# A two-layer hybrid decoder on one core: constants behind the first weights, later transposes at the seam, early products four pairs at a time

## Chip, core and metric

The kernel runs on one core of a Trainium2 chip. The metric is the time on the device of one launch, in microseconds (us). Five engines each work through an instruction list of their own, in order: PE (TensorE, matmuls and transposes), DVE (VectorE), ACT (ScalarE), POOL (GpSimd) and SP (SyncE, which here issues every DMA). A wait of an instruction holds up everything behind it in its engine's list.

## What is computed

Two layers over 1024 tokens of width 1024, in float32. Cut to what matters here:

```
h = RMSNorm_pre(x);  z = h @ W_in                  # conv group and attention group share one projection
m = concat(conv_out, attn_out) @ W_out
x = x + RMSNorm_post(m)                            # the mixer ends here
f = gated MLP(RMSNorm_pre(x)): up 1024 -> 2*2816, causal depthwise conv (3 taps), gate, down 2816 -> 1024
x = x + RMSNorm_post(f)
```

## The kernel before

**Arithmetic.** Every matmul operand is split in two parts, a rounded one and the rest, and every product is three matmuls (`prod`: high by high, low by high, high by low). Weights are loaded by SP into `raw` tiles and split by ACT (the high part) and POOL or DVE (the low part): in the mixer at L459 (load), L463 (ACT) and L469 (POOL), in the up stage at L1409 (load) and in `parts` (L1304, L1305).

**Mixer.** A planner (`Flow`, `fl`) runs Python generators on its own clock and writes the instructions of PE, DVE, ACT and POOL in the order in which it lets them go on; `yield 7.0` means that a generator goes on at about 7 us of that clock. At the start of layer 0 the eight row tiles of x (128 tokens each) are loaded (`first_x`, L242), normalised (`prenorm`: square on ACT L357, a power on POOL L349, scaling on DVE L359) and transposed by PE (L364); ACT copies the high part out of PSUM (L366) and DVE subtracts the low one (L367). A tile k takes two PSUM buffers, and there are two, so that tile k+1 is transposed when DVE has done with tile k. The tiles of x sit in buffers with the tags "y" and "xr", two of each.

**SP's order** is not written by hand. A scheduler places the DMAs by priority, and SP takes them one by one.

**The seam.** The up stage multiplies the normalised rows by 22 pairs of weight tiles in a scheme of seven products for four blocks. One product is a slot: four groups of three matmuls of 128x512, twelve in all. The list `seq` gives the order of slots as pairs (j, n), with j the product and n the weight pair. The right-hand sides are b11 and b21 (tokens of the first half, ready early), b22 (second half), and t1 to t4 (sums of blocks). Eight of the 22 pairs (`EARLY`) have their two products by b11 and b21, "e1" and "e2", put first of all, since those need no token of the second half. e2 adds to the PSUM bank that e1 has left: `e_copy` copies the bank to SBUF (tile `ea`, tag "acc", three buffers) after each of the two, and the copies are stored to DRAM (L1465), to be fetched when their pair's turn comes. Meanwhile the mixer's last four row tiles are finished: on DVE the residual sum (L1172, L1173), on ACT the square (L1178), on POOL the power, on DVE the scaling (L1185, tile `xn`). At the slots `NORM_T` `norm_t` transposes one of these four tiles each on PE (L1357), and in that slot and the three after it `norm_c` makes b22 and t1 to t4 of it: copies out of PSUM by ACT (L1374, L1375), subtractions by DVE (L1372, L1386), high parts by ACT (L1385, L1391). The first slots after the sixteen early ones are (1, 0), which takes the PSUM bank `pO`, and (6, 0), which reads t2.

```
L54    NORM_T = (2, 5, 8, 11)
L55    ACC_BUFS = 3
L1339  seq = [(j, n) for q in range(0, len(early), 2) for j in ("e1", "e2") for n in early[q:q + 2]]
L1459  def e_copy(n, j):
L1461      eh[n] = up.tile([P, T], F32, tag="acc", name="ea", bufs=ACC_BUFS)
L1462      se.activation(eh[n][:, 0:HB], px[n], AF.Copy)
L1465      sy.dma_start(esp[l][n], eh.pop(n))
L1619  px[n] = (pmm.tile([P, HB], F32, tag="mm", name="px") if j == "e1" else
```

PSUM pools: `pmm` has two banks, `pS` three, `ptr` two, `pO` one.

Of the kernel before, what the change touches and what calls it, by code (L numbers as in the profile page):

```python
# [17 lines left out]
P = 128  # L18
D = 1024
T = 1024  # L20
# [30 lines left out]
B_AHEAD = 8  # L51
F_AHEAD = 5
P_AHEAD = 3
NORM_T = (2, 5, 8, 11)  # L54
ACC_BUFS = 3  # L55
E_BUFS = 5
LATE = 12
# [156 lines left out]
def build(tc, ap, out):  # L214
# [7 lines left out]
    with ExitStack() as top:  # L222
# [14 lines left out]
        def const(name, shape, dt=F32):  # L237
            return cst.tile(shape, dt, tag=name, name=name)
# [9 lines left out]
            return t  # L248

        xin = [ap["x"][t * P:(t + 1) * P, :] for t in range(8)]  # L250
        first_x = lambda t: load_x(xin[t], ("y", "y", "xr")[t % 3])
        x0 = [first_x(0)]
        ident = const("ident", [P, P])
        sy.dma_start(ident, ap["ident"])
        identr = const("identr", [P, P], mybir.dt.bfloat16)
        ve.tensor_copy(identr, ident)
        g_pre = gvec(0, 0)
        x0 += [first_x(1), first_x(2)]
        nmask = xs.tile([P, P], F32, tag="m0", name="nmask", bufs=4)
        sy.dma_start(nmask, ap["nmask"])  # L260
        nmaskr = const("nmaskr", [P, P], mybir.dt.bfloat16)
        ve.tensor_copy(nmaskr, nmask)
        cos = const("cosT", [P, 8, 8])
        sy.dma_start(cos, ap["cos"])
        sin = const("sinT", [P, 8, 8])
        sy.dma_start(sin, ap["sin"])
        negh = const("negh", [P, 8])
        ve.memset(negh, -0.5)

        def params(l):  # L270

            li = 0.8 - 0.6 * math.exp(-0.3 * l)

            def ptile(key, shape):
                return par.tile(shape, F32, tag=key, name=f"{key}{l}", bufs=2)

            cw, cv, sg = ptile("cw", [P, 4, CK]), ptile("cv", [P, 3, 4]), ptile("sg", [P, 1])
            sy.dma_start(cw, ap["cw"][l])
            sy.dma_start(cv, ap["cvec"][l])
            sy.dma_start(sg, ap["subg"][l])  # L280
            lv = par.tile([P, 4, HD], F32, tag="lv", name="lv", bufs=1)
            sy.dma_start(lv, ap["lamv"][l:l + 1].broadcast_to([P, 4, HD]))
            cws, hv, ls, nl = ptile("cws", [P, 4, (CK + 1) // 2]), ptile("hv", [P, 2, 4]), ptile("ls", [P, 2]), ptile("nl", [P, 1])
            pars[l] = dict(cw=cw, cws=cws, cv=cv, hv=hv, sg=sg, nl=nl)
            yield
            ve.tensor_scalar(cw, cw, 0.5, None, op0=ALU.mult)
            ve.tensor_copy(cws[:, :, 0], cw[:, :, 0])
            cw2 = cw[:, :, 1:CK].rearrange("p c (m two) -> p c two m", two=2)
            ve.tensor_tensor(cws[:, :, 1:], cw2[:, :, 0], cw2[:, :, 1], op=ALU.add)
            ve.tensor_scalar(hv, cv[:, 1:3, :], 0.5, None, op0=ALU.mult)  # L290
            ve.tensor_scalar(sg, sg, (1.0 - li) * math.sqrt(P), None, op0=ALU.mult)
            ve.tensor_tensor(lv[:, 0:2, :], lv[:, 0:2, :], lv[:, 2:4, :], op=ALU.mult)
            ve.tensor_reduce(ls, lv[:, 0:2, :], axis=AX.X, op=ALU.add)
            se.activation(ls, ls, AF.Exp)
            ve.tensor_tensor(nl, ls[:, 1:2], ls[:, 0:1], op=ALU.subtract)
            ve.tensor_scalar(nl, nl, -li, None, op0=ALU.add)
# [117 lines left out]
        for l in range(DEPTH):  # L414
            xres = xin if l == 0 else x2[l - 1]
            with ExitStack() as st:
# [3 lines left out]
                hh = (hA, hB)  # L420
                if l == 0:
                    for t in range(8):
                        late[t] = prenorm(ptr, x0[t] if t < 3 else first_x(t), g_pre, hh[t // 4], t % 4)
                if l == 0:
                    for _ in params(0):
                        pass
                p = pars[l]
                wm = ap["wmix"][l]

# [840 lines left out]
                def next_params():  # L1270
                    g = params(l + 1)
                    yield 200.0
                    next(g)
                    yield 220.0
                    next(g, None)
                    fl.op("dve", 1.6)

                if l + 1 < DEPTH:
                    fl.spawn(next_params())
                with tc.manual_schedule(engines={mybir.EngineType.PE, mybir.EngineType.DVE,  # L1280
# [4 lines left out]
            with ExitStack() as st:  # L1285
# [44 lines left out]
                with ExitStack() as su:  # L1330
# [5 lines left out]

                    order = [i for k in range(K2) for i in (k, k + K2)]
                    early = EARLY
                    seq = [(j, n) for q in range(0, len(early), 2) for j in ("e1", "e2") for n in early[q:q + 2]]  # L1339
                    for n in range(NFT):  # L1340
                        if n in early:
                            seq += [(4, n - 1)] + [(j, n) for j in (6, 5, 7, 3)]
# [114 lines left out]
                            sy.dma_start(C[n][0][:, h0], esp[l][n][:, HB:T])  # L1457

                    def e_copy(n, j):  # L1459
                        if j == "e1":  # L1460
                            eh[n] = up.tile([P, T], F32, tag="acc", name="ea", bufs=ACC_BUFS)  # L1461
                            se.activation(eh[n][:, 0:HB], px[n], AF.Copy)  # L1462
                        else:
                            se.activation(eh[n][:, HB:T], px[n], AF.Copy)  # L1464
                            sy.dma_start(esp[l][n], eh.pop(n))  # L1465

                    def sums_of(n, j):
                        cg, cv = C[n]
# [144 lines left out]
                    for s, (j, n) in enumerate(seq):  # L1613
# [2 lines left out]
                        if s in before:  # L1616
                            norm_t(before[s])
                        if j in (1, "e1"):
                            px[n] = (pmm.tile([P, HB], F32, tag="mm", name="px") if j == "e1" else  # L1619
                                     pO.tile([P, HB], F32, tag="o", name="px"))  # L1620
                        elif j == 6:
                            py[n] = pS.tile([P, HB], F32, tag="S", name="py")
                        elif j == 5:
                            pz[n] = pS.tile([P, HB], F32, tag="S", name="pz")
# [237 lines left out]
```

## Time and profile before

| | us |
|---|---|
| median of 3 runs | 2316.41 (2315.09 to 2317.93) |
| the profiled execution | 2314.21 |
| its span in the trace | 2312.4 |
| PE busy | 2202.4 (95% of the span) |
| DVE busy | 1879.3 (81%) |
| ACT busy | 1126.7 (49%) |
| POOL busy | 832.6 (36%) |

The mean granted TensorE clock was 0.979 of full speed. The seam of layer 0 runs from about 497 to 554 us, that of layer 1 from 1644 to 1701 us. Of the waits of PE, the one that the words of this case speak of at the seam is that for the transposes (line L1357), and at the start that for the first transposes (line L364).

### The profile page before, as it was taken

To read this page: it belongs to the slowest core of one execution; us is meant where nothing else is said; L and a number is where in the kernel's file an instruction comes from. 1 tells how busy PE (TensorE), PEld (TensorE's weight loads), DVE (VectorE), ACT (ScalarE), POOL (GpSimd) and SP (SyncE) were. 2 spreads that over 40 slices of the span, in tenths; PEclk is the share of its full clock that TensorE was granted. 3 is DMA by queue.
4 is the path that set the end of the run, shared out by engine and by line. 5 is a ranking of instruction groups with operands and counts; after the bars stand their busy time and mean duration, and the time that the engine had idled before them with its cause. 6 is when DMAs were issued, how large, how long until landed. Compare 5 with 4: busy or idle time off the path is not lost. (4 is left out here: it accounts for less than half of the span.)

```text
span 2312.4 us, 31516 instructions
## 1 busy us (share of the span) xinstructions
PE 2202.4 (95%) x10568; PEld 1838.5 (80%) x10568; DVE 1879.3 (81%) x3287; ACT 1126.7 (49%) x2458; POOL 832.6 (36%) x894
## 2 busy tenths in 40 slices
PE   6999997999999999999889999979999999999998
PEld 5898895878877878788778988868788778787886
DVE  6988988667888888777889889896678888887777
ACT  4445456655444444444534545465554444445443
POOL 3324312245444545201533333122454554442024
PEclk9999997999999999999999999979999999999999
DMA  4313323454333343933433123235533343348353
GB/s 156 86 48 92 79 72 123 164 206 138 119 120 130 111 137 130 316 96 111 135 100 103 41 82 97 73 114 191 194 118 124 119 136 123 104 168 274 96 164 118
DMA packets 140129, 295.39 MB, mean 128 GB/s; under 512 B 16832, under 2 KB 33984, under 8 KB 139456
## 3 DMA queue, kind: packets, MB, share of 16 engines
q1 hardware_dynamic: 139968, 293.39, 39.7%
q8 instruction: 83, 1.36, 0.3%
q14 instruction: 78, 0.64, 0.1%
HBM read 198.44 MB, written 78.12 MB: 120 GB/s over the span
## 5 line engine op out<-in xcount | busy, mean ns | idle before, releaser
L1660 PE MATMUL pd<-wp,wo 128*128 128x512 f32 x1776 | 414.2, 395 | 4.8 <-DVE wp L1305 2.8
L1660 PEld LDWEIGHTS pd<-wp,wo 128*128 128x128 f32 x1776 | 333.9, 188 | 81.7 <-DVE wp L1305 3.6
L1609 PE MATMUL py<-t,wo 128*128 128x512 f32 x1584 | 381.8, 394 | 5.8 <-DVE cg L1477 5.8
L1609 PEld LDWEIGHTS py<-t,wo 128*128 128x128 f32 x1584 | 296.8, 188 | 77.4 <-ACT wo L1304 9.0
L1305 POOL TENSOR_TENSOR wo<-ws,wo 128x512 fp32r<-128x512 f32 x176 | 249.9, 1432 | 279.5 <-ACT wo L1304 274.1
L1609 PE MATMUL px<-hA,wo 128*128 128x512 f32 x1056 | 255.3, 394 | 0.0
L1305 POOL TENSOR_TENSOR wo<-raw,wo 128x512 fp32r<-128x512 f32 x132 | 181.4, 1378 | 166.1 <-ACT wo L1304 157.3
L1609 PEld LDWEIGHTS px<-hA,wo 128*128 128x128 f32 x1056 | 198.6, 189 | 44.5 <-ACT ea L1464 0.5
L1305 POOL TENSOR_TENSOR wo<-fa,wo 128x512 fp32r<-128x512 f32 x66 | 103.1, 1577 | 323.0 <-ACT wo L1304 293.9
L1304 ACT ACTIVATE wo<-ws 128x512 fp32r<-128x512 f32 x176 | 108.8, 627 | 136.7 <-PE py L1609 47.4
L1495 DVE SCALAR_TENSOR_TENSOR acc<-cg,fw,acc 128x512 f32<-128x512 f32 x176 | 132.6, 754 | 41.7 <-ACT acc L1483 38.1
L597 DVE SCALAR_TENSOR_TENSOR scr<-u,cw,scr 128x256 f32<-128x256 f32 (+2 forms) x288 | 158.0, 565 | 3.7 <-ACT scr L591 3.6
L852 ACT ACTIVATE e<-S,mxv 128x512 f32<-128x512 f32 (+2 forms) x192 | 110.1, 581 | 64.6 <-DVE mxv L847 41.2
L1483 ACT ACTIVATE acc<-cg,fb,fw 128x512 f32<-128x512 f32 x88 | 68.2, 774 | 148.8 <-DVE cg L1477 148.8
L857 POOL TENSOR_TENSOR sm<-sm 128x1 f32<-128x1 f32 x64 | 25.5, 398 | 316.9 <-ACT e L852 301.6
L499 PE MATMUL pq<-whq,hA 128*128 128x384 f32 x512 | 135.5, 346 | 3.9 <-ACT whq L463 3.9
L499 PE MATMUL pq<-whq,hB 128*128 128x384 f32 x512 | 133.9, 342 | 0.0
L1609 PE MATMUL pz<-b,wo 128*128 128x512 f32 x528 | 129.8, 394 | 1.9 <-DVE cv L1477 1.9
L1609 PE MATMUL pz<-t,wo 128*128 128x512 f32 x528 | 128.7, 392 | 0.0
L1609 PEld LDWEIGHTS pz<-b,wo 128*128 128x128 f32 x528 | 98.4, 188 | 27.4 <-issue 5.1
L843 DVE TENSOR_REDUCE mxv<-S 128x1 f32<-128x512 f32 (+2 forms) x192 | 100.5, 549 | 24.1 <-PE S L827 18.2
L1609 PEld LDWEIGHTS pz<-t,wo 128*128 128x128 f32 x528 | 99.1, 188 | 22.7
(279 smaller groups left out, 5027.2 us busy)
## 6 DMA issues: line engine op xcount, KB each, us to landing
raw<-in_wupd SPq DMA_DIRECT2D x104, 512.0 KB, 3.6
fa<-f SPq DMA_DIRECT2D x154, 256.0 KB, 2.7
f<-fs SPq DMA_DIRECT2D x88, 256.0 KB, 3.3
raw<-in_wmix SPq DMA_DIRECT2D x80, 256.0 KB, 3.0
f<-gg SPq DMA_DIRECT2D x66, 256.0 KB, 2.0
raw<-in_wmix SPq DMA_DIRECT2D x64, 192.0 KB, 2.4
qs<-sth SPq DMA_DIRECT2D x64, 128.0 KB, 2.4
os<-onT SPq DMA_DIRECT2D x16, 512.0 KB, 3.2
```

The lines of the kernel that those rows point to most:

```text
L499: mm = pe.matmul(dst, a, b, start=first and k + j == 0, stop=final and k == n - 1 and j == 2)
L597: ve.scalar_tensor_tensor(dst, src, wk, dst, op0=ALU.mult, op1=ALU.add)
L843: ve.tensor_reduce(mv_[:, j:j + 1], S, axis=AX.X, op=ALU.max, negate=True)
L852: se.activation(e[:, c0:c0 + w], S, AF.Exp, bias=mv_[:, 0:1], accum_out=sm[:, j:j + 1])
L857: po.tensor_tensor(sm[:, 0:1], sm[:, 0:1], sm[:, 1:2], op=ALU.add)
L1304: se.activation(w[:, 0], raw, AF.Copy)
L1305: eng.tensor_tensor(w[:, 1], raw, f32(w[:, 0]), op=ALU.subtract)
L1483: se.activation(acc[n, v, hf], C[n][v][:, 2 + hf * HB:2 + hf * HB + HB], AF.Identity, bias=fb[:, mt:mt + 1], scale=fw[:, mt, 2:3])
L1495: ve.scalar_tensor_tensor(dst, c[:, j + hf * HB:j + hf * HB + HB], fw[:, mt, j:j + 1], a, op0=ALU.mult, op1=ALU.add)
L1609: pe.matmul(ps, x, y, start=first and k + j == 0, stop=k == 3 and j == 2, skip_group_check=not first)
L1660: pe.matmul(ps[tt], x, y, start=first and k + n == 0, stop=k == K2 - 1 and n == 2, skip_group_check=not first)
```

## The change

Three things. **At the start**, the loads of `nmask`, `cos`, `sin` and of the layer's parameters are taken out of the row of first loads and put into a generator `constants` of the mixer's planner; the tiles of x go round "y", "y", "xr", "xr", so that four are loaded at once. **At the seam**, `NORM_T` moves to slots 4, 6, 9 and 12. **The early products** come in groups of four pairs in place of two, in four PSUM banks (two of `pmm`, one of `pO`, one of `pS`), and each `e_copy` takes an "acc" buffer of its own for half a tile and stores 256 KB itself: 16 stores of 256 KB in each layer in place of 8 of 512 KB.

```diff
-NORM_T = (2, 5, 8, 11)
+NORM_T = (4, 6, 9, 12)
...
-        first_x = lambda t: load_x(xin[t], ("y", "y", "xr")[t % 3])
+        first_x = lambda t: load_x(xin[t], ("y", "y", "xr", "xr")[t % 4])
...
-        x0 += [first_x(1), first_x(2)]
-        nmask = xs.tile([P, P], F32, tag="m0", name="nmask", bufs=4)
-        sy.dma_start(nmask, ap["nmask"])
+        x0 += [first_x(1), first_x(2), first_x(3)]
+        nmask = const("nmask", [P, P])
         nmaskr = const("nmaskr", [P, P], mybir.dt.bfloat16)
-        ve.tensor_copy(nmaskr, nmask)
         cos = const("cosT", [P, 8, 8])
-        sy.dma_start(cos, ap["cos"])
         sin = const("sinT", [P, 8, 8])
-        sy.dma_start(sin, ap["sin"])
...
                 if l == 0:
-                    for _ in params(0):
-                        pass
+                    par0 = params(0)
+                    next(par0)
...
+                def constants():
+                    yield 1.0
+                    next(par0)
+                    sy.dma_start(cos, ap["cos"])
+                    sy.dma_start(sin, ap["sin"])
+                    sy.dma_start(nmask, ap["nmask"])
+                    yield 7.0
+                    next(par0, None)
+                    ve.tensor_copy(nmaskr, nmask)
+                    fl.op("dve", 1.8)
+
+                if l == 0:
+                    fl.spawn(constants())
...
-                    seq = [(j, n) for q in range(0, len(early), 2) for j in ("e1", "e2") for n in early[q:q + 2]]
+                    seq = [(j, n) for q in range(0, len(early), 4) for j in ("e1", "e2") for n in early[q:q + 4]]
...
                     def e_copy(n, j):
-                        if j == "e1":
-                            eh[n] = up.tile([P, T], F32, tag="acc", name="ea", bufs=ACC_BUFS)
-                            se.activation(eh[n][:, 0:HB], px[n], AF.Copy)
-                        else:
-                            se.activation(eh[n][:, HB:T], px[n], AF.Copy)
-                            sy.dma_start(esp[l][n], eh.pop(n))
+                        e = up.tile([P, T], F32, tag="acc", name="ea", bufs=ACC_BUFS)[:, 0:HB]
+                        se.activation(e, px[n], AF.Copy)
+                        sy.dma_start(esp[l][n][:, 0:HB] if j == "e1" else esp[l][n][:, HB:T], e)
...
                         if j in (1, "e1"):
-                            px[n] = (pmm.tile([P, HB], F32, tag="mm", name="px") if j == "e1" else
-                                     pO.tile([P, HB], F32, tag="o", name="px"))
+                            q = early.index(n) % 4 if j == "e1" else 2
+                            px[n] = ((pmm if q < 2 else pO if q == 2 else pS)
+                                     .tile([P, HB], F32, tag=("mm", "mm", "o", "S")[q], name="px"))
```

The generator `params` is cut in three by one more `yield`: its tiles, its four loads, its arithmetic. The lines of the kernel move by a few numbers (L1609 becomes L1617, L1357 becomes L1368, L1462 and L1464 become L1472, L1465 becomes L1473).

PE at the seam of layer 0, before (px are the early products, hA_5273 is b11 and hA_5274 is b21, pt the transposes):

```order
1760 L1609 MATMUL px<-hA_5273,wo 128x512 x24
1761 L1357 MATMUL pt<-ident,xn 128x128 x8
1762 L1609 MATMUL px<-hA_5274,wo 128x512 x24
1763 L1609 MATMUL px<-hA_5273,wo 128x512 x12
1764 L1357 MATMUL pt<-ident,xn 128x128 x8
```

and now:

```order
1760 L1617 MATMUL px<-hA_5273,wo 128x512 x48
1761 L1368 MATMUL pt<-ident,xn 128x128 x8
1762 L1617 MATMUL px<-hA_5274,wo 128x512 x24
1763 L1368 MATMUL pt<-ident,xn 128x128 x8
1764 L1617 MATMUL px<-hA_5274,wo 128x512 x24
1765 L1617 MATMUL px<-hA_5273,wo 128x512 x12
1766 L1368 MATMUL pt<-ident,xn 128x128 x8
```

The first transposes stood behind two early products and stand behind four.

ACT at the same place, before (xn<-xe are the squares, ea<-px the copies of early products, ts and b_5734 the first copies of the transposed tile 0):

```order
430 L1178 ACTIVATE xn,ss<-xe 128x1024 x4
431 L1462 ACTIVATE ea<-px 128x512
432 L1304 ACTIVATE wo<-raw 128x512
433 L1462 ACTIVATE ea<-px 128x512
434 L1374 ACTIVATE ts<-pt 128x512
435 L1375 ACTIVATE b_5734<-pt 128x4x128
```

and now:

```order
433 L1175 ACTIVATE xn,ss<-xe 128x1024 x4
434 L1472 ACTIVATE ea<-px 128x512
435 L1315 ACTIVATE wo<-raw 128x512
436 L1472 ACTIVATE ea<-px 128x512
437 L1315 ACTIVATE wo<-raw 128x512
438 L1472 ACTIVATE ea<-px 128x512
439 L1315 ACTIVATE wo<-raw 128x512
440 L1472 ACTIVATE ea<-px 128x512
441 L1385 ACTIVATE ts<-pt 128x512
442 L1386 ACTIVATE b_5734<-pt 128x4x128
```

Four copies of early products, not two, stand ahead of the copies of tile 0.

SP at the same place, before (gb_0_10737 is the gain vector of the next layer, x_0_7 the last row tile's store):

```order
150 L1175 DMA x_0_7_113<-xe 128x1024
151 L247 DMA gb_0_10737<-in_norms 128x1024
152 L1409 DMA raw<-in_wupd 128x1024
153 L1465 DMA e_1_329<-ea 128x1024
154 L1465 DMA e_4_332<-ea 128x1024
```

and now:

```order
147 L1172 DMA x_0_7_111<-xe 128x1024
148 L247 DMA gb_0_10753<-in_norms 128x1024
149 L1473 DMA e_1_327<-ea 128x512
150 L1420 DMA raw<-in_wupd 128x1024
151 L1473 DMA e_4_330<-ea 128x512
152 L1473 DMA e_7_333<-ea 128x512
```

The first early store moves up past one load of weights, and still stands behind the load of the gain vector.

## Rows read from the trace of the kernel before

**Rows 1.** PE's waits: line waited for, us in total, times, longest.
```profile
PE pt L364 <- DVE ss L347: 13.7, 1, 13.7
PE pt L1357 <- DVE ss L347: 7.8, 2, 3.9
PE pq L499 <- POOL wlq L469: 3.8, 9, 0.6
```

**Rows 2.** Timeline, PE, layer 0's seam: start, us, engine, line, operation, count, idle before.
```profile
507.19 1.94 PE L1357 MATMUL pt<-ident,xn 128*128 128x128 f32 x8 [3.88 <-DVE ss L347]
508.79 9.31 PE L1609 MATMUL px<-hA,wo 128*128 128x512 f32 x36
...
527.12 1.03 PE L1357 MATMUL pt<-ident,xn 128*128 128x128 f32 x8
527.91 8.42 PE L1609 MATMUL px<-hA,wo 128*128 128x512 f32 x36
...
553.71 2.96 PE L1609 MATMUL py<-t,wo 128*128 128x512 f32 x12
```

**Rows 3.** Windows: stretch, us, busy by engine (count), granted clock, DMA share, GB/s.
```profile
505.00:510.00 5.00, 2.81 (x11) 2.64 (x12) 4.63 (x8) 4.60 (x10) 3.50 (x4) 0.71 0.73 297
```

**Rows 4.** Timeline, PE, layer 1's seam.
```profile
1644.81 5.60 PE L1609 MATMUL px<-hA,wo 128*128 128x512 f32 x24
...
1700.66 2.96 PE L1609 MATMUL py<-t,wo 128*128 128x512 f32 x12
```

**Rows 5.** Timeline, DVE: last scaling and first subtractions of the seams.
```profile
510.46 2.30 DVE L1185 SCALAR_TENSOR_TENSOR xn<-xe,rs,gb 128x1024 f32<-128x1024 f32 x1 [0.43 <-POOL rs L349]
512.69 0.68 DVE L1372 TENSOR_TENSOR ts<-pt,hA 128x512 f32<-128x512 f32 x1
...
1659.79 0.68 DVE L1372 TENSOR_TENSOR ts<-pt,hA 128x512 f32<-128x512 f32 x1
```

**Rows 6.** Timeline, ACT, layer 0's seam.
```profile
506.94 0.58 ACT L1462 ACTIVATE ea<-px 128x512 f32<-128x512 f32 x1
...
543.49 1.67 ACT L1385 ACTIVATE t<-ts 128x512 fp32r<-128x512 f32 x3
...
546.92 0.62 ACT L1304 ACTIVATE wo<-ws 128x512 fp32r<-128x512 f32 x1
```

**Rows 7.** DMA, 505 to 525 us (median us to landing), then all early stores.
```profile
e<-ea SPq DMA_DIRECT2D x2, 512.0 KB, 6.1
...
gb<-in_norms SPq DMA_DIRECT2D x1, 512.0 KB, 4.7
...
DMA to landing us min/median/max: 2.6/3.1/7.3
```

**Rows 8.** Timeline, SP's DMA issues, layer 0's seam.
```profile
512.79 0.33 SPq L247 DMA_DIRECT2D gb<-in_norms  x1
...
513.69 2.59 SPq L1465 DMA_DIRECT2D e<-ea  x2
```

**Rows 9.** Timeline, DVE, then PE, the start of the kernel.
```profile
11.37 0.23 DVE L262 CAST nmaskr<-nmask 128x128 bf16<-128x128 f32 x1 [6.62 <-DMA nmask<-in_nmask]
...
12.39 1.28 DVE L359 SCALAR_TENSOR_TENSOR xr<-xr,rs,gb 128x1024 f32<-128x1024 f32 x1 [0.73 <-POOL rs L349]
...
17.60 1.28 DVE L367 TENSOR_TENSOR hA<-pt,hA 128x512 fp32r<-128x512 f32 x2
...
13.73 1.97 PE L364 MATMUL pt<-ident,xr 128*128 128x128 f32 x8 [13.73 <-DVE ss L347]
...
25.13 1.67 PE L364 MATMUL pt<-ident,xr 128*128 128x128 f32 x8 [2.44 <-DVE hA L367]
...
28.40 1.12 PE L364 MATMUL pt<-ident,xr 128*128 128x128 f32 x4 [0.38 <-DVE hA L367]
```

**Rows 10.** DMA, issues from 0 to 4 us (median us to landing).
```profile
xr<-in_x SPq DMA_DIRECT2D x3, 512.0 KB, 7.8
gb<-in_norms SPq DMA_DIRECT2D x1, 512.0 KB, 6.9
```

## What I expect, and why

> **What bounds the kernel.** I first read the waits of PE, which is busy for 95% of the span, so that only what PE waits for can be won. The reader is to see three lines that the change touches [rows 1]: 13.7 us before the first transposes of the kernel, 7.8 us in two waits of 3.9 before the first transposes of each seam, and 3.8 us for split weights in the first projections. Then I read PE's timeline through the seam of layer 0 [rows 2]. After two early slots PE stands still for 3.88 us until the first of the four late row tiles is scaled, transposes it, and works on until (6, 0), the first product with t2, starts at 553.71. I use the start of (6, 0) as the mark of each seam. The wait has an after-effect: in the window from 505 to 510 us the mean granted clock is 0.71 of full speed [rows 3], so that after the idle time the lower of the two levels (1.2 and 2.4 GHz) was granted for a part; the eight transposes take 1.94 us there and 1.03 later, and 36 matmuls 9.31 us and later 8.42 [rows 2]. That is 0.9 + 0.9 = 1.8 us beside the 3.88. Layer 1's seam, from its first early product at 1644.81 to (6, 0) at 1700.66 [rows 4], has the other wait of 3.9.
>
> Behind PE runs a second chain. The sums b22 and t1 to t4 are made on DVE, tile after tile. DVE's subtractions of tile 0 start when the last row tile has been scaled, at 510.46 + 2.30 = 512.76 [rows 5], and from there DVE goes on with little idle time to t2 of tile 3. In layer 1 the same subtraction starts at 1659.79 [rows 5], 1147.10 later; both seams are copies of each other up to here.
>
> **Part 1, the transposes later, the four banks, in layer 1.** PE needs nothing of the second half for four slots. A slot is 12 matmuls, 8.42 / 36 x 12 = 2.81 us; four transposes take 527.91 - 527.12 = 0.79 each [rows 2]. Sixteen early slots, (1, 0) and four transposes without a wait are 17 x 2.81 + 4 x 0.79 = 51.0 us, against 1700.66 - 1644.81 = 55.85 [rows 4]: at most 4.8 us are won, the wait and the slower clock together. The number of matmuls, transposes and copies stays. But now DVE's chain is next. (1, 0) takes the bank that e2 of pair 17 had, and the copy of that stands on ACT behind the high parts of t1 to t3 of tile 3 and one more weight split. In layer 0 these high parts run from 543.49 for 1.67 us, and the split of a weight sum ends at 546.92 + 0.62 = 547.54 [rows 6]; the weight sums stand further ahead on DVE now, so I let the split end 1.5 us earlier, at 546.0, and the copy (0.58, as the one at 506.94) at 546.6. (1, 0) then runs from 546.6 and (6, 0) starts at 546.6 + 2.8 = 549.4. In layer 1 that is 549.4 + 1147.1 = 1696.5, a gain of 4.2. I take **-4.2** for layer 1. This holds if DVE's chain starts as before, at 1659.79; ACT's four copies must be through by then. The fourth copy needs the buffer of the first, so it waits until the first half tile is stored. The first copy ends at about 1654.6 (506.94 + 0.58 + 1147.1), and a store takes 3.1 us as the median of all early stores [rows 7]: 1657.8, one copy and the copies of tile 0 behind it, 1659.4. It just fits. With the longest landing, 7.3 [rows 7], it would be 4.2 us later, DVE's chain 3.6 behind what it was, and the gain 0.6; without any wait it is 4.8.
>
> **Part 2, the same seam in layer 0, with a new wait.** Here SP's list differs: ahead of the first early store stands the load of the next layer's gain vector, which overwrites one that the last scaling reads. SP issues it at 512.79, when that scaling is over [rows 5, 8], and it takes 4.7 us [rows 7], to 517.5. Before, nothing at the seam hung on the early stores so soon: the copies of tile 0 stood behind two copies of early products only, and three buffers were enough. Now four copies stand ahead of them, the fourth waits for the first store, and the store is issued behind that load at about 513.2. Behind ACT's fourth copy wait all copies of tile 0, ACT's weight splits, and so DVE's chain. When does the store land? Before, the two stores issued at 513.69 took 6.1 us in the middle [rows 7, 8], with a load of weights also between; the median of all stores is 3.1, the least 2.6 [rows 7]. So it lands between 515.8 and 520.5 (7.3), and I take 518.2, just behind the gain vector and near 513.2 plus the 6.1 less the load that is no longer between. The copy and the first copy of tile 0 follow (0.6 each), and the subtractions start at 519.3 in place of 512.69: the chain is 6.6 us late. By the sum above (6, 0) starts at 549.4 + 6.6 = 556.0 in place of 553.71: +2.3. PE stands still for some 6 us on the way, in two places, so the lower clock can come again, at 0.9 to 1.8 as above; I add 0.5. Layer 0: **+2.8**. The bounds: 4.2 late (store in 2.6 us) and no drop of the clock, -0.1; 8.9 late and one drop of 1.8, +6.4.
>
> The Trainium skill ("DMA: Bandwidth & Descriptors", section "Queues, rings and completion order") says that each DMA engine takes the descriptors of a queue in ring order, and that a completion signal lands only after all earlier writes of that engine. By that rule the store cannot be reported before the gain vector's 517.5, which is the +2.8; without it, with a landing as short as the shortest, the term would be -0.1. The trace bears the rule out in so far as the stores behind that load took 6.1 and not 3.1 us [rows 7].
>
> The sixteen more stores of half the size move the same bytes. DMA issue is not on PE's path outside of this one wait, so I cost them at nothing; the cover is the rest of the seam's slots, which stand between a pair's stores and its turn. Were it gone, PE would wait for a landing of 3.1 us [rows 7].
>
> **Part 3, the start.** Before, DVE's cast of the mask waits for its load until 11.37 and the first scaling stands behind it, so PE's first transposes start at 13.73 [rows 9]. Now that cast comes late. The first scaling then waits for the gain vector, issued in the first two us and 6.9 under way [rows 10], 8.6; the transposes can start at about 10. But each next tile's transposes wait for DVE's subtractions of the one before, which stand behind the scalings of tiles 1 and 2, whose loads take 7.8 us [rows 10] as before. The fourth tile's load goes out with the first ones and no longer behind the first transposes. A scaling takes 1.28 us after a wait of 0.73 for POOL, two subtractions 1.28 [rows 9]; with these, the last of tile 0's subtractions ends at 16.6, and for each tile more come another scaling with its wait, its sum and two subtractions, some 3.5: the fourth tile is transposed at about 23.3 and the fifth at 26.9, where it was 25.13 and 28.40 [rows 9]. Of the four us at the head 1.5 are left, since POOL's powers for tiles 4 and 5 now stand behind weight splits that come earlier. I take **-1.3**; the bounds are +0.5 (one split of POOL more in front) and -3.5 (some of the 3.8 us of waits for split weights [rows 1] go as well). The constants' loads go out behind four loads of weights, and are used much later than they land.
>
> **Sum.** -1.3 + 2.8 - 4.2 = -2.7. The profiled execution took 2314.21 us, so 2311.5; it stands 2.2 under the median, so as a median 2316.4 - 2.7 = **2313.7**. What PE has won it keeps, as it is nearly always busy behind each place.
>
> **Rivals.** (a) *The new wait is hidden.* If the store lands before DVE would start anyway (SP free earlier, or the buffers not in this order), layer 0 wins the 4.3 us of layer 1's reckoning (549.4 against 553.71). With -4.2 and -1.3 to -2.5 for the start this gives -10 to -11, 2306. For it: the gain vector is the only thing in the way. Against: the scheduled order, in which it stands right ahead of the store. (b) *ACT's wait for the store decides in both seams, and the clock drops.* Slower. It decides if the store takes longer than about 4 us in layer 1 too; at 1650 to 1655 us the row tiles' own stores are under way there. At the upper bounds it is +6.4 in layer 0, -0.6 in layer 1, and 0 at the start: +5.8, 2322. For it: the start of DVE's chain in layer 1 has half a us to spare. Against: no gain vector is in the way there. Beside this the Trainium skill ("TensorE: Matmul & The Clock Gate", section "A second HAM failure mode: psum-queue depth-cycling") warns that short pauses of PE between groups in cycling PSUM banks can make its clock go down again and again; no row here shows it apart from the one drop. (c) *The start does nothing*, because POOL holds the fifth tile: the sum is -1.4 and the time 2315.
>
> **Chances.** About 0.2% (4.6 us) is what a measurement can tell from no change. My forecast has 0.55, with (c) in it 0.65: from 2309 to 2318, mostly within 0.2%, and a good fifth of it below 2311.8. (a) has 0.22, all faster. (b) has 0.13, most of it over +4.6. So faster 0.38, same 0.52, slower 0.10. For 8 times in 10 the range reaches from rival (a) at 2306 to 2319.
>
> **What would show it.** Right: in layer 1 no wait before the transposes and (6, 0) some 51 to 52 us after the first early product; in layer 0 ACT idle before its fourth copy, released by a DMA, until about 518, the first subtraction at about 519, and PE idle before the last early slots. Wrong: ACT's fourth copy in layer 0 before 514; or, on the other side, DVE's first subtraction of layer 1 after 1662; at the start, the fifth tile's transposes after 28.4.

## The result, and the profile after

The changed kernel is slower: 2322.26 us in the median of 17 runs (2315.86 to 2330.85) against 2315.67 of the kernel before, measured beside it (17 runs, 2312.26 to 2318.79). The ratio is 1.0031 with a 95% interval of 1.0021 to 1.0041, that is 5 to 9 us more. The forecast was 2313.7 with a range up to 2319.

| | before | after |
|---|---|---|
| span of the profiled execution | 2312.4 | 2327.3 |
| PE busy | 2202.4 (95%) | 2214.0 (95%) |
| DVE, ACT, POOL busy | 1879.3, 1126.7, 832.6 | 1884.0, 1125.4, 834.2 |
| mean granted clock | 0.979 | 0.977 |
| first early product of layer 0 at | 497.71 | 503.72 |
| from there to (6, 0), layer 0 | 56.0 | 61.1 |
| the same in layer 1 | 55.8 | 57.1 |

The profiled execution of the changed kernel, 2329 us, lies near the top of its runs. Its 14.9 us more span are not the median's 6.6: 6.0 of them have come up before the seam of layer 0 begins, in the mixer.

PE's waits, read as [rows 1] (line waited for, us in total, times, longest), now of the changed kernel:

```profile
PE px L1617 <- ACT ea L1472: 11.4, 3, 4.2
PE pt L361 <- DVE hA L364: 9.3, 4, 3.9
PE pt L361 <- DVE xr L356: 9.1, 1, 9.1
...
PE pq L496 <- POOL wlq L466: 3.7, 9, 0.6
```

The 7.8 us before the seams' first transposes are gone, as the change means to have it. In their place stand 11.4 us in three waits of the early products for ACT's copies. At the start the 13.7 us have become 9.1, and the waits between the tiles have grown to 9.3 (they were 6.0).

Where the three waits lie is shown by PE's timeline through both seams [rows 2, 4] in the changed kernel:

```profile
503.72 11.05 PE L1617 MATMUL px<-hA,wo 128*128 128x512 f32 x48
514.61 1.03 PE L1368 MATMUL pt<-ident,xn 128*128 128x128 f32 x8
...
552.65 4.44 PE L1617 MATMUL px<-hA,wo 128*128 128x512 f32 x12 [3.91 <-ACT ea L1472]
560.41 4.61 PE L1617 MATMUL px<-hA,wo 128*128 128x512 f32 x12 [3.32 <-ACT ea L1472]
564.87 0.40 PE L1617 MATMUL py<-t,wo 128*128 128x512 f32 x1
...
1657.43 11.05 PE L1617 MATMUL px<-hA,wo 128*128 128x512 f32 x48
...
1693.83 11.27 PE L1617 MATMUL px<-hA,wo 128*128 128x512 f32 x48
1709.25 5.41 PE L1617 MATMUL px<-hA,wo 128*128 128x512 f32 x12 [4.16 <-ACT ea L1472]
1714.50 2.96 PE L1617 MATMUL py<-t,wo 128*128 128x512 f32 x12
```

Four slots run through, the transposes follow without a wait and at full speed (1.03, not 1.94). But PE then stops behind the last early slots: in layer 1 once, for 4.16 us before (1, 0), in layer 0 twice. The slot behind each stop takes 4.4 to 5.4 us, where the row of a slot at full clock shows 2.96. The windows of the changed kernel [rows 3] say why:

```profile
553.00:561.00 8.00, 4.68 (x14) 3.26 (x13) 7.78 (x10) 6.29 (x13) 5.02 (x4) 0.77 0.25 98
561.00:566.00 5.00, 5.00 (x16) 3.90 (x16) 4.91 (x7) 2.12 (x4) 1.84 (x3) 0.69 0.35 111
...
1709.00:1715.00 6.00, 5.75 (x15) 4.54 (x16) 5.91 (x8) 2.66 (x6) 2.84 (x5) 0.55 0.34 114
```

From 1709 to 1715 the granted clock (the figure behind the engines' busy times) is 0.55, so for nearly all of this stretch the lower of the two levels, right behind the stop.

What PE waited for is on ACT. Its timeline in the changed kernel, first layer 0, then layer 1 [rows 6]:

```profile
512.95 0.58 ACT L1472 ACTIVATE ea<-px 128x512 f32<-128x512 f32 x1
...
524.04 0.60 ACT L1472 ACTIVATE ea<-px 128x512 f32<-128x512 f32 x1 [7.98 <-DMA e<-ea]
...
551.49 0.63 ACT L1315 ACTIVATE wo<-ws 128x512 fp32r<-128x512 f32 x1 [4.04 <-DVE ws L1431]
552.02 0.58 ACT L1472 ACTIVATE ea<-px 128x512 f32<-128x512 f32 x1
552.50 0.62 ACT L1402 ACTIVATE t<-ts 128x512 fp32r<-128x512 f32 x1
...
1672.55 0.60 ACT L1472 ACTIVATE ea<-px 128x512 f32<-128x512 f32 x1 [2.51 <-DMA e<-ea]
...
1700.31 0.64 ACT L1315 ACTIVATE wo<-ws 128x512 fp32r<-128x512 f32 x1 [4.03 <-DVE ws L1431]
...
1708.62 0.57 ACT L1472 ACTIVATE ea<-px 128x512 f32<-128x512 f32 x1
```

and DVE's beside it [rows 5]:

```profile
516.47 2.30 DVE L1182 SCALAR_TENSOR_TENSOR xn<-xe,rs,gb 128x1024 f32<-128x1024 f32 x1 [0.43 <-POOL rs L346]
525.16 0.69 DVE L1383 TENSOR_TENSOR ts<-pt,hA 128x512 f32<-128x512 f32 x1 [6.39 <-ACT ts L1385]
...
1673.67 0.69 DVE L1383 TENSOR_TENSOR ts<-pt,hA 128x512 f32<-128x512 f32 x1 [1.20 <-ACT ts L1385]
...
1699.53 0.69 DVE L1431 TENSOR_TENSOR ws<-ws,raw 128x512 f32<-128x512 f32 x1
1701.98 0.89 DVE L1383 TENSOR_TENSOR t<-ts,t 128x512 fp32r<-128x512 f32 x1 [1.76 <-ACT t L1402]
```

Two things are to be seen. In layer 0 the fourth copy of an early product waits 7.98 us for the store of the first, and DVE's chain starts 6.39 us late; that was forecast. And in both layers ACT waits 4.03 us for a sum of weights (ws) that DVE makes; the copy of t4 of tile 2 and two copies of early products stand behind that split, and DVE then waits 1.76 us for the copy of t4. The two engines hold each other up, and PE waits for the copies. How late DVE is by then is told by the row in which t2's low part of tile 3 is the first subtraction, here of layer 1, in the kernel before and in the changed one:

```profile
1693.23 4.69 DVE L1372 TENSOR_TENSOR t<-ts,t 128x512 fp32r<-128x512 f32 x4
```
```profile
1708.93 2.97 DVE L1383 TENSOR_TENSOR t<-ts,t 128x512 fp32r<-128x512 f32 x3
```

Counted from the first early product this is 48.4 us before and 51.5 now. Before, it lay 7.4 us ahead of (6, 0), and PE did not stop again between its pause and (6, 0).

Why the store of layer 0 is late is shown by SP's issues in the changed kernel, of layer 0 and then of layer 1:

```profile
518.80 0.33 SPq L247 DMA_DIRECT2D gb<-in_norms  x1
519.22 0.38 SPq L1473 DMA_DIRECT2D e<-ea  x1
...
1667.54 1.33 SPq L1473 DMA_DIRECT2D e<-ea  x2
```

In layer 1 the store goes out as soon as the first copy is made (1667.5). In layer 0 the copy is made at 513.5, but the load of the gain vector stands ahead of the store in SP's list and waits for the last scaling, so that the store goes out 5.7 us later.

### The profile page after: what moved, and what is told of

It reads as the page before. It is cut to its first block, busy times and chain, and to the rows that moved or that the text cites. A ratio compares the mean times of both kernels' runs of the same rounds, so it can differ in the third digit from the quotient of the medians.

```text
span 2327.3 us, 31559 instructions
## 1 busy us (share of the span) xinstructions
PE 2214.0 (95%) x10568; PEld 1845.7 (79%) x10568; DVE 1884.0 (81%) x3287; ACT 1125.4 (48%) x2458; POOL 834.2 (36%) x894
## 5 line engine op out<-in xcount | busy, mean ns | idle before, releaser
L1617 PE MATMUL py<-t,wo 128*128 128x512 f32 x1584 | 381.8, 394 | 5.4 <-DVE cg L1485 5.4
L1617 PEld LDWEIGHTS py<-t,wo 128*128 128x128 f32 x1584 | 297.0, 188 | 77.1 <-ACT wo L1315 8.7
L1617 PE MATMUL px<-hA,wo 128*128 128x512 f32 x1056 | 260.0, 399 | 11.4 <-ACT ea L1472 11.4
L1617 PEld LDWEIGHTS px<-hA,wo 128*128 128x128 f32 x1056 | 200.8, 191 | 58.0 <-ACT ea L1472 13.2
L1617 PE MATMUL pz<-b,wo 128*128 128x512 f32 x528 | 129.8, 394 | 1.8 <-DVE cv L1485 1.8
L1617 PE MATMUL pz<-t,wo 128*128 128x512 f32 x528 | 128.8, 392 | 0.0
L1617 PEld LDWEIGHTS pz<-b,wo 128*128 128x128 f32 x528 | 98.4, 188 | 27.3 <-issue 5.0
L1617 PEld LDWEIGHTS pz<-t,wo 128*128 128x128 f32 x528 | 99.1, 188 | 22.7
```

Of the source, the lines that this page charges most:

```text
L1617: pe.matmul(ps, x, y, start=first and k + j == 0, stop=k == 3 and j == 2, skip_group_check=not first)
```

## The experiments

The mark below is the start of (5, 0), the slot behind (6, 0), counted from the first early product, in the one profiled execution of each kernel: where (6, 0) starts in time and then stops inside, the mark of the forecast would not show it. The medians come from four measurements with a kernel before of their own in each; the ratios are to that one. Differences between medians of different measurements, as given below, can therefore be off by about 1 us.

| kernel | median us | ratio to before, 95% interval | mark, layer 0 | mark, layer 1 |
|---|---|---|---|---|
| before | 2314.3 to 2315.7 | | 58.8 | 58.7 |
| the change | 2322.26 | 1.0031 (1.0021 to 1.0041) | 63.9 | 59.9 |
| e1 only the start | 2316.99 | 1.0007 (0.9997 to 1.0018) | 59.8 | 61.2 |
| e2 only the seam | 2321.25 | 1.0021 (1.0012 to 1.0030) | 66.0 | 60.0 |
| e3 half buffers | 2321.99 | 1.0029 (1.0019 to 1.0039) | 62.4 | 59.7 |
| e4 gain vector behind | 2318.44 | 1.0015 (1.0006 to 1.0024) | 58.8 | 59.8 |
| e8 as e4, old slots of the transposes | 2318.19 | 1.0009 (0.9996 to 1.0022) | 59.9 | 58.8 |
| e9 the change, banks anew | 2317.42 | 1.0007 (0.9998 to 1.0016) | 61.5 | 55.8 |
| e5 as e4, banks anew | 2311.57 | 0.9988 (0.9979 to 0.9997) | 57.2 | 57.3 |
| e6 as e5, old start | 2310.50 | 0.9991 (0.9981 to 1.0001) | 57.1 | 57.3 |
| e7 as e6, split later | 2306.69 | 0.9966 (0.9955 to 0.9977) | 56.6 | 54.5 |

**Start and seam apart.** e1 takes the seam's lines of the change (slots, order, copies, banks) back to those of before:

```diff
-NORM_T = (4, 6, 9, 12)
+NORM_T = (2, 5, 8, 11)
...
-                    seq = [(j, n) for q in range(0, len(early), 4) for j in ("e1", "e2") for n in early[q:q + 4]]
+                    seq = [(j, n) for q in range(0, len(early), 2) for j in ("e1", "e2") for n in early[q:q + 2]]
...
```

and e2 the lines of the start:

```diff
-        first_x = lambda t: load_x(xin[t], ("y", "y", "xr", "xr")[t % 4])
+        first_x = lambda t: load_x(xin[t], ("y", "y", "xr")[t % 3])
...
```

> Only the start of the change (loads of the constants behind the first weights, four tiles of x at once); the seams are as before. Theory (the loss is made at the seams, by ACT's fourth copy that waits for a store): -1 to +1 us against the kernel before, both seams as before, 56.0 and 55.9 us from the first early product to (6, 0). Rival (the start shifts the mixer of layer 0 into more stretches at the lower clock, as in the profiled execution, where 7 us were lost between 28 and 504 us): +4 to +7 us.

> Only the seam of the change (later transposes, four pairs in four banks, half tiles stored one by one); the start is as before. Theory (loss at the seams): +5 to +7 us against the kernel before; layer 0's seam 61 us and layer 1's 57, as in the changed kernel. Rival (loss by the start): less than +3 us.

The start alone cannot be told from no change (its interval reaches from 0.7 us faster to 4.2 slower); the seam alone is 3 to 7 us slower. So the loss is made at the seams in the main, as the theory had it; that the start adds a us or two is not excluded. Not as expected: e1's seams were 1 and 2.5 us longer in this execution than those of before, and e2's layer 0 two longer than that of the change. In layer 1 ACT waited 4.57 us there for DVE's ws, in the order of before, and PE 2.47 us for the copy behind it; the block of the two engines is not new with the change, and its size varies. Whether the start shifts the mixer into stretches at the lower clock is looked for in the granted clock. The windows of the kernel before, then of the changed one, then of e1:

```profile
190.00:200.00 10.00, 8.27 (x48) 6.92 (x47) 9.92 (x20) 3.32 (x10) 0.02 (x1) 1.00 0.65 185
225.00:230.00 5.00, 5.00 (x31) 4.75 (x30) 5.00 (x13) 1.62 (x5) 0.20 (x1) 1.00 0.01 2
```
```profile
190.00:200.00 10.00, 8.29 (x39) 6.77 (x38) 9.92 (x20) 3.04 (x9) 0.51 (x3) 0.83 0.66 191
225.00:230.00 5.00, 4.04 (x17) 3.52 (x17) 5.00 (x13) 0.21 (x2) 0.38 (x1) 0.66 0.33 128
```
```profile
190.00:200.00 10.00, 8.29 (x48) 6.91 (x47) 9.92 (x19) 3.43 (x11) 0.00 (x0) 1.00 0.59 175
225.00:230.00 5.00, 5.00 (x26) 4.59 (x25) 4.62 (x13) 1.50 (x5) 0.00 (x0) 0.83 0.00 2
```

The same stretches of the mixer were given full clock in one execution and 0.66 to 0.83 in another, and with the same start (change and e1) not in the same places. From 190 to 200 us PE is busy for 8.3 us in all three, so it has pauses there in each; the clock behind them differs. This is one execution of each kernel; the mean granted clock from 28 to 497 us is 0.97 before and in e1 and 0.96 in the change, which by an estimate from some 440 us of work is about 4 of the us that the change lost there.

**The gain vector in front of the first store.** e4 orders the next layer's gain vector behind the last early store on SP; e3 leaves it and puts two copies in one buffer, so that the fourth copy needs no store.

```diff
-            sy.dma_start(t, ap["norms"][l, i:i + 1].broadcast_to([P, D]))
+            d = sy.dma_start(t, ap["norms"][l, i:i + 1].broadcast_to([P, D]))
+            if gate is not None:
+                after(d, gate)
...
-                        g_pre = gvec(l + 1, 0)
+                        g_pre = gvec(l + 1, 0, est[0])
```

Here `est[0]` is the last early store, and `after` orders a DMA behind another on SP. e3 against the change:

```diff
-                        e = up.tile([P, T], F32, tag="acc", name="ea", bufs=ACC_BUFS)[:, 0:HB]
+                        k = ec[0] % 2
+                        ec[0] += 1
+                        if k == 0:
+                            eh[0] = up.tile([P, T], F32, tag="acc", name="ea", bufs=ACC_BUFS)
+                        e = eh[0][:, k * HB:k * HB + HB]
```

> The change, with the load of the next layer's gain vector ordered behind the last early store on SP, and nothing else. Theory (in layer 0 it is this load that holds the first store): ACT's wait before its fourth copy falls from 8.0 us to the 2.5 of layer 1, layer 0's seam from 61.2 us to 57 as in layer 1, and the time is 4 us under the change, +2 to +3 against the kernel before. Rival (the store is late by the traffic of the other loads and stores at the seam, not by the gain vector): the wait stays at 6 us or more and the time is that of the change.

> The change, with two half tiles in each of the three buffers, so that the fourth copy needs no store (the seventh does). Theory (the wait for the store is the cause): no DMA ahead of ACT's fourth copy, DVE's first subtraction right behind the last scaling in both seams (15.0 us after the first early product), no slower clock behind long waits; the seams take 51 to 53 us and the time is 5 to 10 us under the kernel before, 12 or more under the change. Rival (ACT and DVE hold each other up in tiles 2 and 3, since ACT's splits of weight sums and DVE's subtractions wait in turn, store or not): PE still stops before the last early slots, the seams take 55 to 57, and the time is within 2 us of the kernel before.

e4 does what was expected, in time (3.8 us under the change) and in its place: layer 0's mark falls from 63.9 to 58.8. ACT's fourth copy in e4, layer 0, and PE's slot of (1, 0):

```profile
514.85 0.60 ACT L1475 ACTIVATE ea<-px 128x512 f32<-128x512 f32 x1 [1.53 <-DMA e<-ea]
```
```profile
552.56 4.61 PE L1620 MATMUL px<-hA,wo 128*128 128x512 f32 x12 [3.92 <-ACT ea L1475]
```

The wait of 7.98 is 1.53, DVE starts right behind the last scaling, and PE still stops 3.92 us before (1, 0). e3 went against the theory as it was put. The fourth copy waits for nothing and the subtractions start 15.0 us after the first early product in both layers, but the marks are 62.4 and 59.7 and the time is that of the change. One row of ACT in e3, layer 0:

```profile
522.56 0.63 ACT L1315 ACTIVATE wo<-raw 128x512 fp32r<-128x512 f32 x1 [6.60 <-DMA raw<-in_wupd]
```

Behind the gain vector stands not only the store but the load of raw weights; with the store no longer waited for, ACT waits there. So neither the theory (seams of 51 to 53 us) nor the rival (55 to 57, and a time within 2 us of before) had e3's layer 0 and its time right; PE does still stop before the last early slots, as the rival had it. And layer 1 tells that the wait for the store (2.51) cost nothing there: without it the mark is 59.7 against 59.9. So the first theory, that the wait for the store is the cause, fell for layer 1. The second theory: DVE's chain and ACT's copies set the end of the seam, and PE's pause has only moved, from before the transposes to before (1, 0).

**The pause has only moved.** e8 takes e4 and puts the transposes back.

```diff
-NORM_T = (4, 6, 9, 12)
+NORM_T = (2, 5, 8, 11)
```

> The change with the gain vector behind, and the transposes back at slots 2, 5, 8 and 11. Theory (DVE's chain and ACT's copies set the end of the seam, and the later transposes only move PE's pause): the pause of 3.9 us before the first transposes is back, with the lower clock behind it; PE then comes to (1, 0) at 53 us, after the copy of e2 of pair 17 at 51, and does not pause there; (5, 0) starts 58 to 60 us after the first early product in both seams, as with the later transposes (58.8 and 59.8) and as before (58.8 and 58.7), and the time is within 2 us of the kernel with the gain vector behind (2318.4). Rival (the later transposes have a gain of their own): (5, 0) at 62 us or later, and the time 4 us or more above that.

It came so. PE in e8, layer 0:

```profile
506.09 1.94 PE L1371 MATMUL pt<-ident,xn 128*128 128x128 f32 x8 [3.89 <-DVE ss L347]
...
537.05 16.79 PE L1620 MATMUL px<-hA,wo 128*128 128x512 f32 x72
```

The old pause with its slow transposes is back, the last six slots run in one piece, and the marks are those of e4 within 1.1 us; the ratios (1.0009 and 1.0015) have overlapping intervals. With the old slots t2 of tile 3 also begins earlier, 49.5 and 48.6 us after the first early product against 51.3 and 51.2 in e4: the later transposes themselves make the chain of DVE and ACT end later.

**The bank.** e5 and e9 change which pair has which bank; e5 with the gain vector behind, e9 without.

```diff
-                            q = early.index(n) % 4 if j == "e1" else 2
-                            px[n] = ((pmm if q < 2 else pO if q == 2 else pS)
-                                     .tile([P, HB], F32, tag=("mm", "mm", "o", "S")[q], name="px"))
+                            q = early.index(n) % 4 if j == "e1" else 0
+                            px[n] = ((pO if q == 0 else pmm if q < 3 else pS)
+                                     .tile([P, HB], F32, tag=("o", "mm", "mm", "S")[q], name="px"))
```

> The change with the gain vector behind the early stores, and with the four banks dealt out anew: the first pair of each four, not the third, takes the bank of pO, which (1, 0) needs after the sixteen early slots. Theory (in both seams PE's wait only moved from before the first transposes to before (1, 0), whose bank is freed by ACT's copy of e2 of pair 17, the fifteenth copy, about 51 us after the first early product; the thirteenth is copied at 46, before PE comes there at 47): the wait before (1, 0) and the slower clock behind it go, (6, 0) waits 1 to 2 us for t2, the seams take 52 to 53.5 us where they took 56 and 57, and the time is 2310 to 2313, 3 to 6 us under the kernel before. Rival (DVE's chain of subtractions is the bound, and the wait moves on to (6, 0), with the slower clock): seams of 55 us or more, and the time is at most 2 us under the same kernel with the old banks (2318.4).

> The change with nothing but the banks dealt out anew (the first pair of each four takes the bank that (1, 0) needs); the gain vector stands where it stood. Theory (two causes, one for each layer: the bank in both, the gain vector in layer 0): in layer 1 (5, 0) comes at 57.3 us as with both mended, in place of 59.9; in layer 0 the subtractions still start at 21 us, t2 of tile 3 is late and PE still pauses, (5, 0) at 62 to 64; the time is 2 to 5 us under the change. Rival (the bank is all that counts): layer 0 comes to 58 us too, and the time is 6 us or more under the change.

In both the pause before (1, 0) is gone (in layer 0 of e9 the one before the last early slot stays, 4.62 us), and PE goes on to (6, 0), which waits for t2. In this the rival of e5 was right: the wait moves on to (6, 0). It is shorter, and the rival's times did not come. PE in e5, layer 1:

```profile
1685.67 11.81 PE L1620 MATMUL px<-hA,wo 128*128 128x512 f32 x51
1697.32 0.63 PE L1620 MATMUL py<-t,wo 128*128 128x512 f32 x2
1700.46 4.13 PE L1620 MATMUL py<-t,wo 128*128 128x512 f32 x10 [2.50 <-DVE t L1386]
```

Two matmuls of (6, 0) run, the third needs the low part of t2 and waits 2.50 us, and the other ten take 4.13. That is why the seams are 1 us longer than expected, though the time is what was forecast (2311.57; it is 2.8 us under the kernel before beside it, where 3 to 6 were expected). e9 shows the two causes apart: layer 1 is mended by the bank alone (55.8), layer 0 is not (61.5, half a us less than expected), since there the gain vector still holds DVE until 21.6 us after the first early product. Its time is 4.8 us under the change by the medians and 5.6 by the ratios, at the upper end of the theory's range. That layer 1 came 1.5 us earlier than the 57.3 of e5 is not the bank but the clock, as a row of e9's layer 1 shows:

```profile
1701.11 2.60 PE L1617 MATMUL py<-t,wo 128*128 128x512 f32 x10 [2.51 <-DVE t L1383]
```

The wait is that of e5 (2.50), in the same code, and this time the ten matmuls behind it take 2.60 and not 4.13.

**The start once more, and the split.** e6 is e5 with the start of before. e7 is e6 with one line more: the split of the weight sum for (6, 0) is taken up a slot later.

```diff
-                            at(m - WO_BUFS + 1, lambda x=x: prep(*x))
+                            at(m - WO_BUFS + (2 if m == 2 * len(early) + 1 else 1), lambda x=x: prep(*x))
```

> The same seam (gain vector behind, banks dealt out anew) with the start of the kernel before. Theory (the start gives 1 us at the first projections and it is lost again in the mixer of layer 0, where pauses come to lie so that the clock falls): within 2 us of the same kernel with the new start, or 1 to 2 us faster. Rival (the start's gain of 1 to 1.5 us lasts): 1 to 2 us slower than with the new start.

> The same as the one with the old start, and the split of the weight sum for (6, 0) is taken up one slot later, behind the copy of t4 of tile 2. Theory (ACT's split waits 4.0 us for DVE's sum, and DVE then 1.8 us for the copy of t4 behind it): that idle time of DVE goes, t2 of tile 3 is 1 to 2 us earlier, (6, 0) no longer waits for it, each seam takes 51 to 52 us. Rival (the split is then late): PE waits before (6, 0) for the split weights, and the seams are no shorter.

e5 and e6 have overlapping intervals, so that the start's effect stays under what can be measured here. e7 is the best of all, 0.9966 (0.9955 to 0.9977) of before in 7 runs, some 8 us, and some 15 under the change. DVE and PE of e7, layer 1:

```profile
1680.29 2.49 DVE L1375 TENSOR_TENSOR t<-ts,t 128x512 fp32r<-128x512 f32 x4
1682.69 0.68 DVE L1375 TENSOR_TENSOR ts<-pt,hA 128x512 f32<-128x512 f32 x1
...
1690.96 2.97 DVE L1375 TENSOR_TENSOR t<-ts,t 128x512 fp32r<-128x512 f32 x3
```
```profile
1690.93 0.63 PE L1609 MATMUL py<-t,wo 128*128 128x512 f32 x2
1692.78 2.60 PE L1609 MATMUL py<-t,wo 128*128 128x512 f32 x10 [1.22 <-DVE t L1375]
```

The four subtractions of t1 to t4 of tile 2 run in one piece, DVE's wait of 1.76 us for the copy of t4 is gone, and t2 of tile 3 begins 50.3 us after the first early product (1690.96 against 1640.71) in place of 51.5 (1708.93 against 1657.43 in the change). (6, 0) still waits, 1.22 us here and 1.81 in layer 0, where no wait was expected; the rival, a late split, did not come. The ten matmuls take 2.60 here, which is worth 1.5 us beside the 1.3 of the shorter wait, but in layer 0 of the same kernel they take 4.14. After e9's 2.51 us with full clock, the lower clock cannot be put down to the length of such short waits: that part of e7's gain in layer 1 may be luck of the one execution.

## Why the prediction was wrong

- **What bounds the kernel.** Right for the kernel before: PE stopped nowhere between the pause and (6, 0), and t2 of tile 3 was begun 7.4 us ahead. DVE's chain was named as the second chain and the next bound, but was carried over as it stood. With the later transposes it ends some 3 us later (t2 of tile 3 at 51.5 us after the first early product, before 48.4; in e4, where DVE starts in time, 51.2), and ACT's copies with it. From the first subtraction to t2 of tile 3 it takes 36.2 us in layer 1 of e4 and 33.4 before; 1.2 of these 2.7 us are the longer wait for the copy of t4 (1.76 against 0.56), and where the rest comes from is not shown.
- **Part 1, layer 1: -4.2 forecast, +1.2 measured** at the same mark, (6, 0) (57.1 against 55.85). This is the step that failed. The copy of e2 of pair 17 was let end at 546.6, 48.9 us after the first early product; it ended at 1709.2, 51.8 after it. I had moved ACT's split of the weight sum forward by 1.5 us because the sum stands further ahead on DVE. In fact ACT waits for an earlier sum (4.03 us), and what stands behind its split (the copy of t4, the copies of early products) holds DVE for 1.76 us; the high parts of tile 3, behind which the copy of pair 17 stands, start 49.1 us after the first early product (1706.53), before 45.8 (543.49 in layer 0). That the bank of this copy is one that (1, 0) needs was seen, and it is new: before, no early product used `pO`. And the pause before (1, 0) was taken as a wait alone; it brought the lower clock with it. From the start of (1, 0) to that of (6, 0) are 5.25 us in place of 2.81. Of the miss of 5.4 us, 2.4 are this clock and 2.9 the late copy. (The landing of the first store was summed to 1657.8 for 1657.7, and 17 slots with four transposes to 51.0 for 50.9; neither matters.) The store that was to take 3.1 us took 4.9 to landing (issued at 1667.54 by SP, ACT went on at 1672.55), and DVE started 16.2 and not 15.0 us after the first early product; but in e3, without that wait and with DVE at 15.0, (6, 0) comes only 0.2 us earlier (56.8 against 57.1), so that this counts for little.
- **Part 2, layer 0: +2.8 forecast, +5.1 measured.** The mechanism was right, and its times to 0.2 us: with the layer's shift of 6.0 taken off, the store landed at 518.0 (forecast 518.2) and the subtractions began at 519.15 (forecast 519.3). e4 shows that it is the gain vector that holds it. Two sizes were off by 1.1 us each: the copy that (1, 0) waits for ended at 560.36, 1.1 later than counted from DVE's start, since the chain to t2 of tile 3 took 34.9 us, before 33.6; and the clock behind the stop cost 1.6 us (560.41 to 564.87 for one slot) where 0.5 was added.
- **The rule on the queue.** The Trainium skill's sentence on ring order and completion ("DMA: Bandwidth & Descriptors", "Queues, rings and completion order") was used to choose the side of the bounds: a landing behind that of the gain vector, not 2.6 us after the issue. The trace agrees in the order: the gain vector landed 4.5 us after its issue (518.80 + 4.5 = 523.3), the store 4.7 after its own (519.22 + 4.7 = 523.9). But stores with no gain vector ahead took 4.9 (layer 1) and 3.9 us (layer 0 of e4), so that the rule's own share stays under 1 us and is not shown. What the gain vector is seen to cost is the wait on SP, 5.7 us before the issue, and this the prediction had (513.2; measured 519.22 less 6.0).
- **Part 3, the start: -1.3 forecast.** The transposes came nearly as counted (9.05 where 10 was counted; the fifth tile at 27.32 where 26.9 was, 1.1 earlier than before), and nothing of it was left at the seam of the profiled execution. "What PE has won it keeps" was the step that failed here. e1 bounds the start at -0.7 to +4.2 us (ratio 0.9997 to 1.0018). In the seven profiled executions with the new start the first early product of layer 0 comes at 496.6 to 503.7 us, in the four with the old one at 496.9 to 499.4; that the lower clock in the mixer makes this difference is likely from the windows above, and not shown.
- **Rival (b)** had the right sign and half of the mechanism: the clock drops in both seams. That its time, 2322, is nearly the one measured is luck: it puts layer 1 at -0.6, which came at +1.2, and the start at 0. Its other half, that the store decides in layer 1 too, is refuted by e3. "TensorE: Matmul & The Clock Gate" of the Trainium skill (section "A second HAM failure mode: psum-queue depth-cycling") warned of short, frequent pauses between groups in cycling banks. Here the lower clock followed single stops of 3.3 to 4.2 us (windows at 0.55 to 0.77), so the trace shows the price of such a drop and not the pattern that the page describes. The price deserved a term in the sum and not only a rival of 0.13.

The misses nearly add up: 5.4 us in layer 1, 2.3 in layer 0 and, by e1's ratio, some 3 at the start are 10.7, and the time came 9.9 above the forecast (7.2 slower by the ratio, where 2.7 faster was forecast). Two things make the loss at the seams, each shown by a run that alters nothing else: the store behind the gain vector in layer 0 (e4), and the late copy of a bank that (1, 0) needs (e9).

Still open: why the chain is longer with the later transposes beside the wait for t4, and why the clock drops behind a pause in one execution and not in another, in the mixer and behind the waits of 1.6 to 2.5 us at (6, 0). No run here steers that.

## What to carry to other kernels

A pause that is removed from one place is won only if the chain behind it still ends ahead of PE in the new order: count from the last producer to the last consumer through every engine, in the new order, and see where PE would meet it next. Where a second engine's list mixes copies that free banks with splits that wait for a third engine, the copy is as late as the split; the cheapest cure here was to choose which buffer is needed first, one line, and the next one to move one split behind the copy. And a pause of PE can cost what the clock behind it costs as well, in the change 1.5 to 2.4 us beside stops of 3.3 to 4.2; behind waits of 1.6 to 2.5 us it was 1.5 in some and nothing in others.

## What was not expected of the hardware

The spread of the changed kernel's runs is 15 us, that of the kernel before 6.5 beside it and up to 10.5 in the later measurements, with the same count of instructions on PE; in the profiled executions the granted clock differs in the same stretches of the mixer (0.66 to 1.00); that this makes the spread is not shown. Behind waits of about 2.5 us at the same place, in the same code, ten matmuls took 4.13 us in e5 and 2.60 in e9 (granted clock from 1700 to 1705 us 0.66 and 1.00). And one DMA that waits for an engine holds more than the next in line: at the seam of layer 0 it held a store in the change (7.98 us of ACT's time) and a load of weights in e3 (6.60), so that taking away the one wait brought the other.
